# Modulation columns of the first four chunks from TensorE, for latents and context in one product

## The chip, the core and the metric

The kernel runs on one core of one Trainium2 chip. The metric is the time of one execution on the device in microseconds (us), and the figure of a kernel is the median of its runs.

## What is computed

Two layers of a diffusion backbone work on 1024 latent tokens and 256 context tokens of width 1024. What matters here is the beginning of layer 0: the modulation and the first product of its mixer.

```python
mod_lat = (silu_c @ ada_w[i] + ada_b[i])[:, None, :]
mod_ctx = (silu_cc @ ada_w[i] + ada_b[i])[None, None, :]
sh1, sc1, g1, sh2, sc2, g2 = jnp.split(mod_lat, 6, axis=-1)
csh1, csc1, cg1, csh2, csc2, cg2 = jnp.split(mod_ctx, 6, axis=-1)
h = modulate(rms_norm(x, norm_g[i, 0]), sh1, sc1)
hc = modulate(rms_norm(ctx, norm_g[i, 0]), csh1, csc1)
...
z = jax.nn.gelu(h @ w_in)
```

`modulate(h, shift, scale)` is `h * (1 + scale) + shift`. Shift and scale of layer 0 are two vector-matrix products of length 1024 with a matrix of 1024 x 2048 (the first two of the six parts of ada_w), once for the latents and once for the context. `h @ w_in` follows for 1280 rows and 4096 columns.

## The kernel before

The tokens are ten tiles of 128 rows: 0 to 7 are latents, 8 and 9 context. The first mixer is a gMLP, called for five tiles at a time. Its products run in the f32r type as three matmuls per piece: high part by high part, low by high, high by low (`mm3`). The width of 1024 is cut into eight chunks of 128, numbered k.

The program begins with a head (lines 676 to 780), which is written out by hand and whose instructions on VectorE, ScalarE, TensorE and the queue of SyncE keep the order of the code (`pins`, line 584). It normalizes the first five tiles of x and makes the first column block, 512 of the 2048 columns of the v half of `h @ w_in`. For each chunk k it does this:

- `flip_x(k)` (line 645): five 128x128 transposes on TensorE into a psA bank. Of the two psA buffers one holds a sum of the head all the time, so the next chunk's flip has to wait until `x_hi(k)` has read the other.
- The modulation columns of the chunk, one number per partition for shift and scale, written into `modc` by `finish_cols` on VectorE (line 198).
- `x_hi(k)` on ScalarE (line 651): scale, shift and the cast to the high part. `x_lo(k)` on VectorE (line 659): the low part.
- `head_mm(k, part)` (line 662) for parts 0 to 2: five 128x512 matmuls each, with the weights that `w_load`, `w_hi` and `w_lo` have loaded and split.

The columns come from `AdaBlock(k0, nk)` (line 588) for nk chunks at once: chunk 0, chunk 1, then pairs. The constructor loads the block's columns of ada_w in tiles "act" (six buffers), `accum` multiplies row block k by its 128 numbers of silu(c) and adds it up on VectorE, and `total` sums the result over the partitions with a matmul by a column of ones (`ones` in the rows), one per chunk and per shift or scale.

After the head `gmlp` (line 823) makes three more column blocks of four u steps each (30 matmuls of 128x512 per u step) and then the rest. Between its steps it takes steps of the generator `extra`, 1 or 2 per u step (18 in these three blocks) and two per feature block after that. The generator begins with the context's modulation, `ada_steps(0, 0, (1,))` and `ada_steps(0, 1, (1,))`. Each of these loads 1024x1024 of ada_w in eight steps of 512 KB into the three buffers "raw", which the weights of w_in use too, adds up on VectorE into `acc`, and ends with small matmuls or transposes and `finish_cols`: 9 steps each. Then come the gate `ada_steps(0, 2, (0, 1))` for both streams, which ends in matmuls with a matrix of ones (`ada_gate`, line 220), and sums for layer 1. In `between` run the preparations of small tables, such as `cwcols`, which are transposed into psA and copied by VectorE (`cols_of`, line 166). The order of these instructions on each engine is made by a scheduler.

Of the kernel before, what the change touches and what calls it, by code (L numbers as in the profile page):

```python
# [32 lines left out]
def hybrid_kernel(  # L33
# [23 lines left out]
    V, S, G, T = Engine(nc.vector, "V"), Engine(nc.scalar, "S"), Engine(nc.gpsimd, "G"), Engine(nc.tensor, "T")  # L57
# [23 lines left out]
    def t_raw():  # L81
        return sb.tile([P, 1024], F32, name=nm("raw"), tag="raw", bufs=3)
# [34 lines left out]
    def t_acc():  # L117
        return stage_pool["pool"].tile([P, 1024], F32, name=nm("acc"), tag="acc", bufs=2)
# [14 lines left out]
    def psB(shape=(P, 512)):  # L133
        return ps.tile(list(shape), F32, name=nm("psB"), tag="psB", bufs=4)
# [192 lines left out]
    def src_row(stage, t):  # L327
        if stage == 0:
            return x_in[0, t * P:(t + 1) * P, :] if t < 8 else ctx_in[0, (t - 8) * P:(t - 7) * P, :]
        return xs[stage][t * P:(t + 1) * P, :]  # L330
# [254 lines left out]
    pA0 = psA()  # L585
    pl0 = [psB() for _ in range(4)] + [pA0[:, 0, :]]

    class AdaBlock:
        def __init__(self, k0, nk):
            self.k0, self.nk = k0, nk  # L590
# [28 lines left out]
                             start=True, stop=True)  # L619

        def finish(self):
            k0, nk = self.k0, self.nk
            p = pts[k0][:, 1, 256:256 + 2 * nk]
            for s in (1, 0):
                finish_cols(0, s, 0, p[:, s * nk:(s + 1) * nk], slice(k0, k0 + nk))

    raws, w0, pts, tms = {}, {}, {}, {}

    def w_load(u, nb=0):
        raws[nb, u] = t_raw()  # L630
        Q.dma_start(raws[nb, u].rearrange("p (a b) -> p a b", a=2),
                    w_in[0][u * 256:u * 256 + 2 * P, E + nb * 512:E + nb * 512 + 512]
                    .rearrange("(k p) n -> p k n", p=P))

    def w_hi(u, nb=0):
        hi, lo = t_w("wh"), t_w("wl")
        w0[nb, u] = (hi.rearrange("p (a b) -> p a b", a=2), lo.rearrange("p (a b) -> p a b", a=2))
        S.copy(hi, raws[nb, u])
        raws[nb, u] = (raws[nb, u], hi, lo)

    def w_lo(u, nb=0):
        raw, hi, lo = raws.pop((nb, u))
        V.tensor_sub(lo, raw, hi)

    def flip_x(k):
        pts[k] = psA()
        for i in range(5):
            T.transpose(out=pts[k][:, i // 4, (i % 4) * P:(i % 4 + 1) * P], in_=xn0[:, i, k * P:(k + 1) * P],
                        identity=ident)

    def x_hi(k):
        pt, tm = pts[k], t_tmp()
        gg, sh = mod_cols(0, 1, 0)[:, k:k + 1], mod_cols(0, 0, 0)[:, k:k + 1]
        S.activation(tm[:, 0:512], pt[:, 0, :], AF.Identity, bias=sh, scale=gg)
        S.activation(tm[:, 512:640], pt[:, 1, 0:128], AF.Identity, bias=sh, scale=gg)
        S.copy(hk(hb0, 0, k)[:, 0:640], tm[:, 0:640])
        tms[k] = tm

    def x_lo(k):
        V.tensor_sub(hk(hb0, 1, k)[:, 0:640], tms[k][:, 0:640], hk(hb0, 0, k)[:, 0:640])  # L660

    def head_mm(k, part):
        wh, wl = w0[0, k // 2]
        a, b = ((0, 0), (0, 1), (1, 0))[part]
        for i in range(5):
            T.matmul(pl0[i], hk(hb0, b, k)[:, i * P:(i + 1) * P], (wh, wl)[a][:, k % 2, :],
                     start=(k == 0 and part == 0), stop=(k == KD - 1 and part == 2))
# [5 lines left out]
        V.tensor_copy(cl, p)  # L673
        return cl

    b0 = AdaBlock(0, 1)
    adab, aR = load_rows([ada_b.rearrange("l (k p) -> (l k) p", p=P)])
    ngr, nR = load_rows([norm_g.rearrange("l i (k p) -> (l i k) p", p=P)])
    for i, t in enumerate(LAT):
        Q.dma_start(xn0[:, i, :], src_row(0, t))  # L680
    w_load(0)
    b1 = AdaBlock(1, 1)
    abcols = cols_in(adab, aR, "abcols")
    ngcols = cols_in(ngr, nR, "ngcols")
    b0.accum(range(KD))
    for i, t in enumerate(LAT):
        r = rstd_of(xn0[:, i, :])
        V.tensor_scalar(out=xn0[:, i, :], in0=xn0[:, i, :], scalar1=r, scalar2=None, op0=ALU.mult)
    flip_x(0)
    b0.total()  # L690
    w_hi(0)
    b0.finish()
    x_hi(0)
    w_lo(0)
    flip_x(1)
    b1.accum(range(0, 4))
    x_lo(0)
    b2 = AdaBlock(2, 2)
    head_mm(0, 0)
    b1.accum(range(4, 8))  # L700
    b1.total()
    b2.accum(range(0, 2))
    b1.finish()
    head_mm(0, 1)
    head_mm(0, 2)
    x_hi(1)
    b2.accum(range(2, 4))
    w_load(1)
    b3 = AdaBlock(4, 2)
    flip_x(2)  # L710
    x_lo(1)
    w_hi(1)
    b2.accum(range(4, 7))
    head_mm(1, 0)
    head_mm(1, 1)
    w_lo(1)
    b2.accum(range(7, 8))
    b2.total()
    head_mm(1, 2)
    b3.accum(range(0, 1))  # L720
    b2.finish()
    x_hi(2)
    b3.accum(range(1, 3))
    x_lo(2)
    w_load(2)
    b4 = AdaBlock(6, 2)
    flip_x(3)
    x_hi(3)
    b3.accum(range(3, 5))
    x_lo(3)  # L730
    w_hi(2)
    head_mm(2, 0)
    head_mm(2, 1)
    head_mm(2, 2)
    flip_x(4)
    head_mm(3, 0)
    b3.accum(range(5, 7))
    w_lo(2)
    b3.accum(range(7, 8))
    head_mm(3, 1)  # L740
    b3.total()
    b4.accum(range(0, 1))
    b3.finish()
    head_mm(3, 2)
    x_hi(4)
    b4.accum(range(1, 3))
    x_lo(4)
    w_load(3)
    flip_x(5)
    x_hi(5)  # L750
    b4.accum(range(3, 5))
    x_lo(5)
    head_mm(4, 0)
    head_mm(4, 1)
    head_mm(4, 2)
    flip_x(6)
    w_hi(3)
    head_mm(5, 0)
    head_mm(5, 1)
    b4.accum(range(5, 8))  # L760
    b4.total()
    w_lo(3)
    b4.finish()
    head_mm(5, 2)
    x_hi(6)
    x_lo(6)
    w_load(0, 1)
    flip_x(7)
    x_hi(7)
# [848 lines left out]
    def pre_b0():  # L1618
# [1 line left out]
        return build(hold["h"], 0, 0, 0, [(0, 5 * P, 3 * P), (3 * P, SEQ, 256)], [], 640)  # L1620

    gmlp(0, hb0, LAT, gate_of(0, 2),
         chain(ada_steps(0, 0, (1,)), ada_steps(0, 1, (1,)), ada_steps(0, 2, (0, 1)), ada_steps(1, 3, (0,)),
               ada_steps(1, 4, (0,))),
         chain(more_cols(), prep_ws(), flip0()), pre_b0, head=(pl0, w0_next))

# [494 lines left out]
```

## Time and profile before

| | |
|---|---|
| three runs | 2856.6 us median (2850.05 to 2860.5) |
| profiled execution | 2860.88 us, its span 2859.1 us |
| granted clock of TensorE, mean | 0.988 |
| TensorE matmul busy | 2741.8 us, 96% |
| VectorE busy | 2221.8 us, 78% |
| ScalarE busy | 1391.2 us, 49% |
| moved by DMA | 537.13 MB |

The profile is one execution, recorded by instruction; the durations in the text are from it. PE is TensorE (PEld its weight loads), DVE VectorE, ACT ScalarE, POOL GpSimd, SP SyncE, and SPq is the queue of SyncE, which issues DMAs. A row of the timeline gives start, duration, engine, line, operation, output <- inputs, shapes and count; in brackets stands how long the engine was idle before and what ended that. Buffers carry the names of the code's tiles. Line 50 is the helper through which every instruction is made.

### The profile page before, as it was taken

Reading aid. Unit: us, or ns where it says so; the run is one execution under the profiler, and the core shown is the slowest. Engines: PE = TensorE matmul, PEld = TensorE weight load, DVE = VectorE, ACT = ScalarE, POOL = GpSimd, SP = SyncE. Lnnn points to the kernel's source line nnn. Section 1 sums busy time; section 2 is a strip of 40 time slices with the busy share of each in tenths; the row PEclk is TensorE's granted clock in tenths of the full one; section 3 lists DMA queues with packets and bytes.
Section 4 is the critical chain, followed back from the end, with each engine's and each line's share of the span. In section 5 each row is a group of like instructions: output and inputs, shape, how many; then the busy total and the mean of one; then the engine's idle time right before and its main releaser. Section 6 shows DMA issues by size and latency. Waiting matters only on the chain.

```text
span 2859.1 us, 40314 instructions
## 1 busy us (share of the span) xinstructions
PE 2741.8 (96%) x14570; PEld 2354.1 (82%) x14570; DVE 2221.8 (78%) x3466; ACT 1391.2 (49%) x2291; POOL 616.6 (22%) x806
## 2 busy tenths in 40 slices
PE   7999999999989999999999899999998999999998
PEld 5798887898889888888788778888887888888786
DVE  6567684787779899887776568898887788888776
ACT  4333242232367444455434545777876444445433
POOL 1164021360210212111000124543333121220000
PEclk9999999999999999999999999999999999999999
DMA  7775457554488355467855565347577345545753
GB/s 260 251 234 166 145 161 227 177 167 131 171 249 240 103 170 162 157 217 238 287 169 184 188 212 186 115 145 239 181 242 220 126 162 182 160 144 198 248 177 125
DMA packets 436335, 537.13 MB, mean 188 GB/s; under 512 B 20004, under 2 KB 300452, under 8 KB 436135
## 3 DMA queue, kind: packets, MB, share of 16 engines
q1 hardware_dynamic: 379575, 470.84, 51.4%
q10 hardware_dynamic: 55408, 59.52, 6.2%
q0 software_dynamic: 1152, 4.19, 0.4%
q8 instruction: 115, 1.88, 0.3%
q14 instruction: 85, 0.70, 0.1%
HBM read 414.40 MB, written 120.07 MB: 187 GB/s over the span
## 4 chain that ended last, share of the span: by engine, by line
PE 65%; DVE 13%; DMA 11%; ACT 5%; issue 4%; POOL 2%; SPq 1%; ACTq 0%; DVEq 0%; POOLq 0%
PE psB L50 48%; PE psA L50 16%; DVE row L50 3%; DVE wl L50 3%; DMA raw<-in_ada_w_dram 3%; DVE tmp L50 1%; DVE acc L50 1%; ACT wh L50 1%; ACT tmp L50 1%; DMA xT<-row 1%; DMA raw<-in_a_w_in_dram 1%; DVE y L50 1%; POOL sm L50 1%; DMA raw<-in_f_w_up_dram 1%; DMA raw<-in_f_w_down_dram 1%
## 5 line engine op out<-in xcount | busy, mean ns | idle before, releaser
L50 PE MATMUL psB<-cmb,wh 128*128 128x512 f32 (+2 forms) x2584 | 750.3, 374 | 7.2 <-ACT row L50 6.2
L50 PEld LDWEIGHTS psB<-cmb,wh 128*128 128x128 f32 x2584 | 471.9, 188 | 98.4 <-ACT row L50 8.1
L50 PE MATMUL psB<-cmb,wl 128*128 128x512 f32 (+2 forms) x1292 | 483.2, 374 | 0.2 <-DVE wl L50 0.2
L50 ACT CAST wh<-raw 128x1024 fp32r<-128x1024 f32 (+1 forms) x313 | 265.1, 863 | 441.6 <-PE psB L50 165.5
L50 DVE TENSOR_TENSOR wl<-raw,wh 128x1024 fp32r<-128x1024 f32 (+1 forms) x313 | 307.6, 997 | 106.6 <-ACT wh L50 104.9
L50 PEld LDWEIGHTS psB<-cmb,wl 128*128 128x128 f32 x1292 | 243.2, 188 | 44.0 <-DVE wl L50 0.8
L50 PE MATMUL psB<-wh,big 128*128 128x512 f32 x816 | 271.1, 398 | 3.7 <-ACT big L50 1.3
L50 ACT CAST wh<-row 128x1024 fp32r<-128x1024 f32 (+1 forms) x196 | 162.5, 834 | 186.8 <-DVE row L50 92.3
L50 PE MATMUL psB<-wh,act 128*128 128x512 f32 x640 | 200.1, 390 | 0.8 <-DVE tmp L50 0.8
L50 DVE TENSOR_TENSOR wl<-row,wh 128x1024 fp32r<-128x1024 f32 (+1 forms) x196 | 185.2, 948 | 12.2 <-ACT wh L50 11.8
L50 PE MATMUL psA<-big,wh 128*128 128x320 f32 x1024 | 193.2, 310 | 0.3 <-ACT row L50 0.3
L50 POOL TENSOR_TENSOR row<-raw,raw 128x512 f32<-128x512 f32 x44 | 68.5, 1558 | 574.2 <-DMA raw<-in_f_w_up_dram 490.8
L50 PEld LDWEIGHTS psB<-wh,big 128*128 128x128 f32 x816 | 154.3, 190 | 39.9 <-ACT tmp L50 2.4
L50 DVE SCALAR_TENSOR_TENSOR acc<-raw,ccols,acc 128x1024 f32<-128x1024 f32 x98 | 126.7, 1311 | 75.8 <-DMA raw<-in_ada_w_dram 75.5
L50 DVE SCALAR_TENSOR_TENSOR row<-row,cwcols,row 128x1024 f32<-128x1024 f32 (+2 forms) x142 | 152.6, 1075 | 39.2 <-ACT row L50 22.7
L50 ACT CAST ah<-raw 128x1024 fp32r<-128x1024 f32 x80 | 77.6, 974 | 201.6 <-PE psB L50 80.8
L50 DVE TENSOR_TENSOR row<-row,row 128x512 f32<-128x512 f32 (+4 forms) x169 | 155.9, 926 | 19.9 <-DMA row<-actd 12.2
L50 POOL TENSOR_SCALAR row<-row,sm,sm 128x128 f32<-128x128 f32 x160 | 144.1, 919 | 115.2 <-DMA row<-vscr 99.3
L50 PEld LDWEIGHTS psA<-big,wh 128*128 128x128 f32 x1024 | 159.9, 188 | 0.7 <-ACT row L50 0.5
L50 PE MATMUL psB<-wl,big 128*128 128x512 f32 x408 | 157.2, 395 | 0.9 <-DVE wl L50 0.9
L50 DVE TENSOR_TENSOR al<-raw,ah 128x1024 fp32r<-128x1024 f32 x80 | 90.2, 1128 | 71.9 <-ACT ah L50 71.6
L50 PE MATMUL psB<-row,wh 128*128 128x256 f32 x744 | 136.9, 286 | 8.2 <-ACT wh L50 6.7
(279 smaller groups left out, 6226.0 us busy)
## 6 DMA issues: line engine op xcount, KB each, us to landing
raw<-in_f_w_up_dram SPq DMA_DIRECT2D x121, 512.0 KB, 4.8
raw<-in_ada_w_dram SPq DMA_DIRECT2D x88, 512.0 KB, 4.4
raw<-in_a_w_in_dram SPq DMA_DIRECT2D x64, 512.0 KB, 4.8
wh<-woscr SPq DMA_DIRECT2D x48, 512.0 KB, 4.1
row<-actd SPq DMA_DIRECT2D x44, 512.0 KB, 5.5
actc<-row SPq DMA_DIRECT2D x44, 512.0 KB, 4.1
raw<-actc SPq DMA_DIRECT2D x40, 512.0 KB, 3.6
actd<-row SPq DMA_DIRECT2D x39, 512.0 KB, 2.7
```

The costliest lines, as they stand in the source:

```text
L50: ins = fn(*a, **kw)
```

## The change

Four things change.

The columns of chunks 0 to 3 come from the new `AdaColumn(k0)`, one chunk each. It loads the chunk's columns of ada_w in two tiles of 512 KB (scale first). Its `total` is 8 matmuls for scale and 8 for shift, which add up over the row blocks in PSUM: the stationary operand is a 128x128 piece of ada_w, the moving one two columns, silu(c) and silu(c_ctx) of that row block. So the context's columns of these chunks come out of the same products; `finish(1)` writes them. Chunks 4 to 7 keep `AdaBlock` in two pairs.

In the code of the head ada_b, norm_g and x are loaded ahead of the first column's tiles, and the calls stand in another order. `w_hi(0)` casts in two halves, behind `x_hi(0)`.

The context's part of the generator is now `ctx_steps()`, which sums only columns 512 to 1023 of shift and scale, both in one accumulator: 9 steps where there were 18. All that follows in the generator comes nine steps earlier.

```diff
+    def ctx_steps():
+        acc = t_acc()
+        for k in range(KD):
+            raw = t_raw()
+            for m in range(2):
+                Q.dma_start(raw[:, m * 512:(m + 1) * 512], ada_w[0, k * P:(k + 1) * P, m * D + 512:(m + 1) * D])
+            cc = ccols[:, KD + k:KD + k + 1]
+            if k == 0:
+                V.tensor_scalar(out=acc, in0=raw, scalar1=cc, scalar2=None, op0=ALU.mult)
+            else:
+                V.scalar_tensor_tensor(out=acc, in0=raw, scalar=cc, in1=acc, op0=ALU.mult, op1=ALU.add)
+            yield
+        p = psB()
+        for k in range(KD):
+            T.matmul(p[:, k:k + 1], acc[:, k * P:(k + 1) * P], ones[:, 0:1], start=True, stop=True)
+        for m in range(2):
+            finish_cols(0, m, 1, p[:, 4 * m:4 * m + 4], slice(4, KD))
+        yield
...
+    class AdaColumn:
+        def __init__(self, k0):
+            self.k0, self.nk, self.rv = k0, 1, {}
+            for s in (1, 0):
+                self.rv[s] = t_act((P, KD, P), F32)
+                Q.dma_start(self.rv[s], ada_w[0, :, s * D + k0 * P:s * D + (k0 + 1) * P]
+                            .rearrange("(k p) n -> p k n", p=P))
+
+        def total(self):
+            p = pts[self.k0][:, 1, 256:260]
+            both = ccols.rearrange("p (s k) -> p s k", k=KD)
+            for s in (1, 0):
+                for k in range(KD):
+                    T.matmul(p[:, 2 * s:2 * s + 2], self.rv[s][:, k, :], both[:, :, k], start=(k == 0), stop=(k == KD - 1))
+
+        def finish(self, stream=0):
+            p = pts[self.k0][:, 1, 256:260]
+            for s in (1, 0):
+                finish_cols(0, s, stream, p[:, 2 * s + stream:2 * s + stream + 1], slice(self.k0, self.k0 + 1))
...
-        S.copy(hi, raws[nb, u])
+        for c in ((0, 512), (512, 1024)) if (nb, u) == (0, 0) else ((0, 1024),):
+            S.copy(hi[:, slice(*c)], raws[nb, u][:, slice(*c)])
...
-    b0 = AdaBlock(0, 1)
     adab, aR = load_rows([ada_b.rearrange("l (k p) -> (l k) p", p=P)])
     ngr, nR = load_rows([norm_g.rearrange("l i (k p) -> (l i k) p", p=P)])
     for i, t in enumerate(LAT):
         Q.dma_start(xn0[:, i, :], src_row(0, t))
+    b0 = AdaColumn(0)
     w_load(0)
-    b1 = AdaBlock(1, 1)
+    b1 = AdaColumn(1)
+    b2 = AdaColumn(2)
...
-         chain(ada_steps(0, 0, (1,)), ada_steps(0, 1, (1,)), ada_steps(0, 2, (0, 1)), ada_steps(1, 3, (0,)),
+         chain(ctx_steps(), ada_steps(0, 2, (0, 1)), ada_steps(1, 3, (0,)),
                ada_steps(1, 4, (0,))),
```

What this does to the order of the instructions is shown at three places. The first is TensorE at the beginning of the head. `ident,y` are the transposes of a chunk, the products of 128x1 or 128x2 are the columns, and the 128x512 ones are a part of `head_mm`. Before:

```order
L50 MATMUL psA_186<-ident,y_109 128x128 x5
L50 MATMUL psA_186<-ones,acc_121 128x1 x2
L50 MATMUL psA_208<-ident,y_109 128x128 x5
L50 MATMUL psB_111<-wh_196,big_205 128x512
L50 MATMUL psB_112<-wh_196,big_205 128x512
L50 MATMUL psB_113<-wh_196,big_205 128x512
L50 MATMUL psB_114<-wh_196,big_205 128x512
L50 MATMUL psA_110<-wh_196,big_205 128x512
L50 MATMUL psA_208<-ones,acc_139 128x1 x2
```

And now:

```order
L50 MATMUL psA_176<-ident,y_109 128x128 x5
L50 MATMUL psA_176<-ccols,act_124 128x2 x8
L50 MATMUL psA_176<-ccols,act_126 128x2 x8
L50 MATMUL psB_111<-wh_211,big_204 128x512
L50 MATMUL psB_112<-wh_211,big_204 128x512
L50 MATMUL psB_113<-wh_211,big_204 128x512
L50 MATMUL psB_114<-wh_211,big_204 128x512
L50 MATMUL psA_110<-wh_211,big_204 128x512
L50 MATMUL psA_229<-ident,y_109 128x128 x5
L50 MATMUL psA_229<-ccols,act_130 128x2 x8
L50 MATMUL psA_229<-ccols,act_132 128x2 x8
```

Sixteen products stand where two stood, ahead of the first wide matmul and again behind it, and the second chunk's transposes have moved behind the first five wide matmuls.

The second place is VectorE near the end of the second column block, around the last copy of `cwcols`, whose psA buffer the third block's sum takes next. Products `acc<-raw,ccols` are steps of the modulation sums, each waiting for a load. Before:

```order
L50 SCALAR_TENSOR_TENSOR acc_608<-raw_885,ccols,acc_608 128x1024
L50 COPY cwcols_696<-psA_694 128x66
L50 TENSOR_TENSOR wl_833<-raw_830,wh_832 128x1024
L50 TENSOR_SCALAR acc_942<-raw_943,ccols 128x1024
L50 BN_STATS st_538<-tmp_752 128x6
L50 BN_STATS st_538<-tmp_756 128x6
L50 BN_STATS st_538<-tmp_760 128x6
L50 COPY cwcols_739<-psA_737 128x66
```

And now:

```order
L50 SCALAR_TENSOR_TENSOR acc_645<-raw_870,ccols,acc_645 128x1024
L50 COPY cwcols_736<-psA_734 128x66
L50 TENSOR_TENSOR wl_877<-raw_874,wh_876 128x1024
L50 SCALAR_TENSOR_TENSOR acc_645<-raw_929,ccols,acc_645 128x1024
L50 BN_STATS st_575<-tmp_795 128x6
L50 BN_STATS st_575<-tmp_799 128x6
L50 BN_STATS st_575<-tmp_803 128x6
L50 COPY cwcols_780<-psA_778 128x66
```

The last copy has a sum ahead of it in both; before it was the first of the next set, now it is the last of the context's.

The third place is TensorE at the end of the fourth column block. `psA<-ident,row` are transposes of a token tile, and `psA<-big` begins the next part of the gMLP. Before:

```order
L50 MATMUL psA_1029<-wh_1159,big_485 128x512
L50 MATMUL psA_1254<-ident,row_1193 128x128 x8
L50 MATMUL psB_1270<-ident,acc_942 128x128 x4
L50 MATMUL psB_1276<-ident,acc_942 128x128 x4
L50 MATMUL psA_1321<-big_205,wh_1219 128x320 x2
```

And now:

```order
L50 MATMUL psA_1080<-wh_1213,big_512 128x512
L50 MATMUL psA_1309<-ident,row_1247 128x128 x8
L50 MATMUL psB_1334<-wh_1330,ones 128x512
L50 MATMUL psB_1334<-wl_1331,ones 128x512
L50 MATMUL psB_1338<-wh_1330,ones 128x512
L50 MATMUL psB_1338<-wl_1331,ones 128x512
```

Where the transposes of the context's scale sums stood, the gate's matmuls stand now, which need the high and low parts of its sums.

More of the change, by code (lines that the diff above doesn't have):

```diff
@@ L586, in hybrid_kernel, with finish_block @@
     pl0 = [psB() for _ in range(4)] + [pA0[:, 0, :]]
+    def finish_block(block):
+        k0, nk = block.k0, block.nk
+        p = pts[k0][:, 1, 256:256 + 2 * nk]
+        for s in (1, 0):
+            finish_cols(0, s, 0, p[:, s * nk:(s + 1) * nk], slice(k0, k0 + nk))
     class AdaBlock:
@@ L621, in finish @@
         def finish(self):
-            k0, nk = self.k0, self.nk
-            p = pts[k0][:, 1, 256:256 + 2 * nk]
+            finish_block(self)
+    class AdaColumn:
+        def __init__(self, k0):
+            self.k0, self.nk, self.rv = k0, 1, {}
             for s in (1, 0):
-                finish_cols(0, s, 0, p[:, s * nk:(s + 1) * nk], slice(k0, k0 + nk))
+                self.rv[s] = t_act((P, KD, P), F32)
[11 more added lines that the diff above has]
+                finish_cols(0, s, stream, p[:, 2 * s + stream:2 * s + stream + 1], slice(self.k0, self.k0 + 1))
     raws, w0, pts, tms = {}, {}, {}, {}
@@ L680, in hybrid_kernel @@
         Q.dma_start(xn0[:, i, :], src_row(0, t))
+    b0 = AdaColumn(0)
     w_load(0)
-    b1 = AdaBlock(1, 1)
+    b1 = AdaColumn(1)
+    b2 = AdaColumn(2)
     abcols = cols_in(adab, aR, "abcols")
     ngcols = cols_in(ngr, nR, "ngcols")
-    b0.accum(range(KD))
     for i, t in enumerate(LAT):
@@ L690, in hybrid_kernel @@
     b0.total()
-    w_hi(0)
     b0.finish()
     x_hi(0)
+    b0.finish(1)
+    w_hi(0)
+    x_lo(0)
     w_lo(0)
+    b3 = AdaColumn(3)
+    w_load(1)
+    head_mm(0, 0)
     flip_x(1)
[L696 to L700, printed above, removed]
     b1.total()
-    b2.accum(range(0, 2))
     b1.finish()
+    x_hi(1)
+    b1.finish(1)
     head_mm(0, 1)
     head_mm(0, 2)
[L706 to L709, printed above, removed]
+    x_lo(1)
+    b4 = AdaBlock(4, 2)
     flip_x(2)
-    x_lo(1)
+    b2.total()
+    b2.finish()
+    x_hi(2)
+    b2.finish(1)
     w_hi(1)
-    b2.accum(range(4, 7))
+    b4.accum(range(0, 2))
     head_mm(1, 0)
     head_mm(1, 1)
+    head_mm(1, 2)
+    x_lo(2)
     w_lo(1)
[L717 to L724, printed above, removed]
     w_load(2)
-    b4 = AdaBlock(6, 2)
+    b6 = AdaBlock(6, 2)
     flip_x(3)
+    b3.total()
+    b3.finish()
     x_hi(3)
-    b3.accum(range(3, 5))
-    x_lo(3)
-    w_hi(2)
+    b3.finish(1)
+    b4.accum(range(2, 4))
     head_mm(2, 0)
@@ L734, in hybrid_kernel @@
     head_mm(2, 2)
+    x_lo(3)
+    b4.accum(range(4, 8))
+    w_hi(2)
     flip_x(4)
     head_mm(3, 0)
-    b3.accum(range(5, 7))
+    head_mm(3, 1)
+    b4.total()
+    b4.finish()
+    x_hi(4)
     w_lo(2)
[L739 to L743, printed above, removed]
     head_mm(3, 2)
-    x_hi(4)
-    b4.accum(range(1, 3))
     x_lo(4)
+    b6.accum(range(0, 2))
     w_load(3)
@@ L750, in hybrid_kernel @@
     x_hi(5)
-    b4.accum(range(3, 5))
     x_lo(5)
+    b6.accum(range(2, 5))
     head_mm(4, 0)
@@ L757, in hybrid_kernel @@
     w_hi(3)
+    b6.accum(range(5, 8))
     head_mm(5, 0)
+    b6.total()
+    b6.finish()
+    x_hi(6)
+    w_lo(3)
+    x_lo(6)
     head_mm(5, 1)
[L760 to L763, printed above, removed]
     head_mm(5, 2)
-    x_hi(6)
-    x_lo(6)
     w_load(0, 1)
```

## Prediction

> **What bounds the kernel now.** I began with the page's span and busy times, and went on to the waits of TensorE and to the table by stage.
>
> ```profile
> span 2859.1 us, 40314 instructions
> PE 2741.8 (96%) x14570; PEld 2354.1 (82%) x14570; DVE 2221.8 (78%) x3466; ACT 1391.2 (49%) x2291; POOL 616.6 (22%) x806
> ```
> ```profile
> PE psA L50 <- DVE cwcols L50: 4.6, 1, 4.6
> PE psB L50 <- DVE tmp L50: 2.8, 4, 0.9
> PE psB L50 <- DVE wl L50: 1.7, 2, 1.1
> PE psB L50 <- DVE y L50: 1.3, 1, 1.3
> PE psA L50 <- ACT row L50: 0.3, 1, 0.3
> ```
> ```profile
> 23.00:32.00 9.00, 7.77 (x20) 5.78 (x21) 8.16 (x17) 2.82 (x5) 0.00 (x0) 1.00 0.94 318
> 32.00:66.00 34.00, 32.45 (x164) 25.67 (x163) 26.26 (x42) 17.27 (x25) 0.00 (x0) 1.00 0.67 217
> 96.00:104.00 8.00, 3.48 (x9) 2.81 (x10) 3.60 (x6) 0.00 (x0) 0.00 (x0) 0.79 0.65 223
> ```
> TensorE is busy 96% of the span, so work added to it lengthens the kernel unless it falls where TensorE idles. The second view (us waited, times, longest) covers 60 to 400 us: 10.7 us of waits in all, 4.6 of them one wait for the copy of cwcols. The third (stretch, length, busy us of PE, weight loads, DVE, ACT, POOL, then granted clock, DMA share, GB/s) shows that from 32 to 66 us, where the change puts its matmuls, TensorE works 32.45 of 34 us. There is little idle time there to take anything in. The two kernels issue the same sequences again from about the end of the first gMLP call (some 400 us), so the sum is over 0 to 400 us. Next, the timeline of TensorE in and behind the head (start, us, operation, instructions).
>
> ```profile
> 19.44 0.47 PE L50 MATMUL psA<-ident,y 128*128 128x128 f32 x1 [0.99 <-DVE y L50]
> 19.71 0.85 PE L50 MATMUL psA<-ones,acc 128*128 128x1 f32 x4
> 20.43 1.31 PE L50 MATMUL psA<-ident,y 128*128 128x128 f32 x5
> 23.08 2.08 PE L50 MATMUL psB<-wh,big 128*128 128x512 f32 x4 [1.34 <-ACT big L50]
> 24.95 0.63 PE L50 MATMUL psA<-wh,big 128*128 128x512 f32 x1
> 26.73 1.02 PE L50 MATMUL psA<-ones,acc 128*128 128x1 f32 x4 [1.15 <-DVE acc L50]
> 27.61 2.05 PE L50 MATMUL psB<-wh,big 128*128 128x512 f32 x4
> 33.65 1.09 PE L50 MATMUL psB<-wh,big 128*128 128x512 f32 x4
> 34.57 0.40 PE L50 MATMUL psA<-wh,big 128*128 128x512 f32 x1
> 45.08 0.95 PE L50 MATMUL psA<-ones,acc 128*128 128x1 f32 x8
> 45.88 1.17 PE L50 MATMUL psB<-wl,big 128*128 128x512 f32 x4
> 65.07 0.39 PE L50 MATMUL psA<-wl,big 128*128 128x512 f32 x1
> 100.52 0.79 PE L50 MATMUL psA<-wh,big 128*128 128x512 f32 x1 [4.58 <-DVE cwcols L50]
> 103.60 0.40 PE L50 MATMUL psB<-wl,big 128*128 128x512 f32 x1
> 127.67 1.95 PE L50 MATMUL psB<-ones,acc 128*128 128x1 f32 x16
> 129.48 0.48 PE L50 MATMUL psB<-wl,big 128*128 128x512 f32 x1
> ```
> Paces are read from start to start. A 128x512 matmul takes (24.95-23.08)/4 = 0.47 us early and (34.57-33.65)/4 = 0.23 later: TensorE starts at half pace (the granted clock column reads 1.00 there, so only the pace shows it). Every 128x128 by 128x1 product in f32 is two instructions. One costs (45.88-45.08)/8 = 0.10 or (129.48-127.67)/16 = 0.113 at full pace, and 0.18 (19.71 to 20.43) to 0.22 (26.73 to 27.61) at half. The head's last matmul starts at 65.07.
>
> **The head, part by part.** The other engines' rows, ScalarE first, then VectorE, then the queue of SyncE:
>
> ```profile
> 9.96 1.06 ACT L50 ACTIVATE tmp<-y 128x1024 bf16<-128x1024 f32 x1 [5.60 <-DMA y<-in_x_dram]
> 17.15 1.04 ACT L50 CAST wh<-raw 128x1024 fp32r<-128x1024 f32 x1
> 21.14 1.13 ACT L50 ACTIVATE tmp<-psA,modc 128x512 f32<-128x512 f32 x2 [2.94 <-DVE modc L50]
> 22.30 0.72 ACT L50 CAST big<-tmp 128x640 fp32r<-128x640 f32 x1
> ```
> ```profile
> 36.55 1.53 DVE L50 SCALAR_TENSOR_TENSOR acc<-act,ccols,acc 128x512 f32<-128x512 f32 x2
> 91.39 1.28 DVE L50 SCALAR_TENSOR_TENSOR acc<-raw,ccols,acc 128x1024 f32<-128x1024 f32 x1 [4.12 <-DMA raw<-in_ada_w_dram]
> 97.80 0.75 DVE L50 TENSOR_SCALAR acc<-raw,ccols 128x1024 f32<-128x1024 f32 x1 [3.86 <-DMA raw<-in_ada_w_dram]
> 100.26 0.21 DVE L50 COPY cwcols<-psA 128x66 f32<-128x66 f32 x1
> 163.74 1.28 DVE L50 SCALAR_TENSOR_TENSOR acc<-raw,ccols,acc 128x1024 f32<-128x1024 f32 x1 [5.10 <-DMA raw<-in_ada_w_dram]
> 222.54 1.23 DVE L50 TENSOR_TENSOR wl<-acc,wh 128x1024 fp32r<-128x1024 f32 x1 [3.40 <-ACT wh L50]
> ```
> ```profile
> 1.52 2.05 SPq L50 DMA_DIRECT2D act<-in_ada_w_dram x4
> 3.62 0.50 SPq L50 DMA_DIRECT2D tmp<-in_ada_b_dram  x1
> 4.16 0.59 SPq L50 DMA_DIRECT2D tmp<-in_norm_g_dram  x1
> 4.79 3.15 SPq L50 DMA_DIRECT2D y<-in_x_dram  x5
> ```
> Earlier x. ScalarE begins on the first tile of x at 9.96, after 5.60 us of waiting for its load. The four loads of ada_w (2.05 us of issue, 1 MB) no longer stand ahead of ada_b, norm_g and x on SyncE, so x is issued 2.1 us earlier. At the 318 GB/s of the table that megabyte takes 3.3 us, so the last transpose of flip_x(0) comes 2.1 to 3.3 us earlier: 16.1 to 17.3, I take 16.6. GpSimd's memset and selects of the mask now stand between the first x tiles' statistics; they are over before the last tile, so nothing.
>
> First column. b0's sums on VectorE go (eight, beside waiting). In their place TensorE does 16 products, 32 instructions, at half pace 0.18 to 0.22: 6.4 us, to 23.0. As many bytes as before stand ahead of these tiles, which landed under x's time then, so no wait for them. From the end of the small products to the first 128x512 there were 23.08-20.43 = 2.65 us; now the half cast of wh comes behind x_hi(0) (1.04/2), so 3.2. head_mm(0, 0) then starts at 26.2 and not 23.08: **+3.1** (between +2 and +4).
>
> The other columns. Behind head_mm(0, 0) there were 4 + 3 x 8 = 28 small instructions. Now there are 3 x 32 + 2 x 8 = 112. 84 more at 0.10 to 0.113 are 8.4 to 9.5 us: **+9.0**. TensorE is in order and nearly gapless here, so nothing hides them. What they take off VectorE had only made TensorE wait 1.15 us at 26.73.
>
> Half pace. Before, 15 matmuls of 0.47 instead of 0.23 and some small ones lost 3.8 us. Full pace came at about 31.9, 5.2 us after the last gap. Now it finds 5 wide matmuls, a flip and some small products: 0 to 3.6 lost, I take 2.0: **-1.8**. The Trainium skill, page "TensorE: Matmul & The Clock Gate", Part 1, says that the array leaves half rate after one window of about 3.4 us of sustained work. By that rule the 6.4 us of the first column would already raise the clock, and the sum would be 2 us lower; no run so far shows whether such small products count as work.
>
> Waits. The waits of 1.15 at 26.73 and of about half a us each at flips fall (some 2.2 us). A new one comes: b6.total now stands behind one part of head_mm(5), and six sums of 1.53/2 us stand between x_lo(5) and it on VectorE. TensorE gets there 5.0 us after flip_x(5) (four parts of 1.14, one flip), VectorE in 3.0 + 4.5 = 7.5 (the 3.0 are a flip of 0.5, 1.13 and 0.72 on ScalarE and a difference of under 1): 2.5 us. **0** together. Context's three short operations per column, the earlier tables of ada_b and norm_g, and w_load(1) ahead of the two-column blocks have slack of microseconds on their engines.
>
> Head: 3.1 + 9.0 - 1.8 = **+10.3 us** (+6.5 to +12).
>
> **Behind the head.** Context's sums: 16 loads of 512 KB and 16 sums (1.28 each) become 8 steps, each still one 512 KB buffer, in two DMAs. VectorE gains 10 us, TensorE loses eight transposes, about **-0.9**. The wait at 95.9 us: it costs 4.58 and a slow restart: 7 matmuls in 103.60-100.52 = 3.08 us instead of 1.6, so 6.1. The copy that ends it stands behind an ada_w sum that waited 3.86 us for its load; in the new order one such sum still stands ahead of it, of 1.28 rather than 0.75. Eight ada_w loads through the three buffers come ahead of the copy instead of nine. Between all 6.1 gone and 1.5 more, I take **-2.5**. The gate of ada 2: it moves by nine steps to the end of the fourth column block. Its hi and lo need the last two sums (1.28 each), two casts and two differences (1.23 each). Before, the last sum there ran at 163.74 after 5.10 us of waiting for a load, and the transposes hardly waited. In-order TensorE would now wait between 0 and 4.6 us; **+1.5**. Waits from 166 to 400 us: 6.1 us, and the later steps find VectorE less loaded; at best all go, at worst 2 more come: **-1.5**.
>
> Sum: 10.3 - 0.9 - 2.5 + 1.5 - 1.5 = +6.9 us. The profiled execution took 2860.9 us (span 2859.1 and 1.8 around), so 2867.8; the median of the three runs, 2856.6, lies 4.3 lower, so the forecast is **2863.5 us**, 0.24% more. A measurement of this kernel can tell about 0.5% (14.3 us) from no change: this is no change by that measure.
>
> **The rivals.** A: the small products are paid for. The long wait goes whole with its restart (-6.1), those behind 166 us too (-6.1), the gate is hidden, the transposes go (-0.9), and the head comes out at its low end, +6.5: -6.6, or 2850. For: half the bytes of context's sums. Against: a sum still stands ahead of the copy.
>
> B: slower, TensorE stays at half pace. If streams of one- and two-column products do not count as work, four columns of them between the wide parts could hold the pace down until the last column. The place is from head_mm(0, 0) to head_mm(2, 0), it decides if the pace is still 0.47 at head_mm(1, 0). Price: 30 wide matmuls by 0.24 and 96 small ones by 0.09 are 15.8, of which 2.0 are counted: +13.8, 2877.3, slower by 0.7%. For: the early transposes and small products did not raise the pace before 31.9. Against: ten wide ones from 27.6 on did.
>
> C: the small products hide. Weight loads overlap matmuls; in 32 to 66 us they were busy 25.67 of 34. If most of the 9.0 went beside the wide ones, the head would be +3 and the sum 2856. Against: the eight at 45.08 took their 0.80 us between two wide groups in full.
>
> **How the numbers follow.** The forecast has 0.64 (its own range 2857 to 2871), A 0.14, B 0.10, C 0.12. The range 2850 to 2873 holds forecast, A and C but for their edges, and leaves B out. Faster by over 0.5% (under 2842.3) needs more than A: 0.02. Slower by over 0.5% (above 2870.9) is most of B and the forecast's edge: 0.12. Within: 0.86.
>
> **What would show it.** Right: in the new trace the first 128x512 matmul starts near 26 us, each column's 32 instructions take 3.2 to 3.6 us at full pace, and the head ends near 75 us. The wait for cwcols is there, shorter. Wrong: a head that ends before 70, small products of far less than 0.10 us, wide matmuls at 0.47 beyond 35 us (B), or a difference that arises behind 400 us, where I expect none.

## The result and the profile after

| | before | after |
|---|---|---|
| median of the timed runs | 2851.1 us (6 runs, 2846.2 to 2860.5) | 2875.4 us (6 runs, 2873.9 to 2881.3) |
| profiled execution, its span | 2860.9, 2859.1 us | 2875.3, 2873.5 us |

The changed kernel takes 1.0085 times as long (interval 1.0065 to 1.0104): 24.3 us more, slower by 0.85%. The forecast was +6.9 us and "no change"; the time lies above the range.

I read the new trace in the order of the prediction. First TensorE in the head (start, us, operation, instructions, idle time before it):

```profile
16.40 0.47 PE L50 MATMUL psA<-ident,y 128*128 128x128 f32 x1 [0.99 <-DVE y L50]
16.67 6.83 PE L50 MATMUL psA<-ccols,act 128*128 128x2 f32 x32
26.52 2.07 PE L50 MATMUL psB<-wh,big 128*128 128x512 f32 x4 [3.03 <-ACT wh L50]
28.40 0.63 PE L50 MATMUL psA<-wh,big 128*128 128x512 f32 x1
29.89 6.82 PE L50 MATMUL psA<-ccols,act 128*128 128x2 f32 x32
36.57 2.05 PE L50 MATMUL psB<-wh,big 128*128 128x512 f32 x4
42.04 3.71 PE L50 MATMUL psA<-ccols,act 128*128 128x2 f32 x32
45.62 2.05 PE L50 MATMUL psB<-wh,big 128*128 128x512 f32 x4
47.47 0.63 PE L50 MATMUL psA<-wh,big 128*128 128x512 f32 x1
51.26 3.63 PE L50 MATMUL psA<-ccols,act 128*128 128x2 f32 x32
54.76 1.17 PE L50 MATMUL psB<-wh,big 128*128 128x512 f32 x4
56.10 1.91 PE L50 MATMUL psB<-wh,big 128*128 128x512 f32 x4
73.63 1.05 PE L50 MATMUL psA<-ones,acc 128*128 128x1 f32 x8 [2.05 <-DVE acc L50]
84.06 0.39 PE L50 MATMUL psA<-wl,big 128*128 128x512 f32 x1
```

The beginning is as forecast: last transpose at 16.40, first wide matmul at 26.52. But the second column still takes 36.57-29.89 = 6.68 us, 0.21 an instruction, so half pace. The wide matmuls of the first chunk behind it are at half pace too. The third column is at full pace (45.62-42.04 = 3.58 us, 0.11 each), and right behind it the wide ones take (47.47-45.62)/4 = 0.46 us again. The same comes once more behind the fourth column, at 56.10. The head's last matmul starts at 84.06 instead of 65.07: +19.0 us.

The stretches of the same trace say why (stretch, length, busy us and instructions of PE, weight loads, DVE, ACT, POOL, then granted clock, DMA share, GB/s):

```profile
42.00:45.40 3.40, 3.40 (x33) 3.40 (x31) 0.00 (x0) 0.00 (x0) 0.00 (x0) 1.00 0.07 14
45.40:48.80 3.40, 3.40 (x12) 2.72 (x12) 1.66 (x8) 2.47 (x4) 0.00 (x0) 0.53 0.90 283
55.60:59.00 3.40, 3.40 (x10) 2.71 (x9) 2.32 (x6) 2.65 (x4) 0.00 (x0) 0.54 0.87 275
```

From 42.0 to 45.4 us TensorE does nothing but small products, without a gap. In the next 3.4 us the granted clock is 0.53. So the clock falls although the engine never idles.

Next, four of the nine rows of its waits from 60 to 400 us (us in all, times, longest), and the two places of the timeline that the prediction spoke of, with the longest wait last:

```profile
PE psB L50 <- DVE tmp L50: 7.3, 6, 3.9
PE psA L50 <- DVE acc L50: 2.0, 1, 2.0
PE psA L50 <- DVE wl L50: 1.6, 1, 1.6
PE psA L50 <- DVE cwcols L50: 0.4, 1, 0.4
```
```profile
116.87 0.50 PE L50 MATMUL psA<-wh,big 128*128 128x512 f32 x1 [0.41 <-DVE cwcols L50]
179.78 0.50 PE L50 MATMUL psB<-wh,ones 128*128 128x512 f32 x1 [0.35 <-ACT tmp L50]
181.31 0.50 PE L50 MATMUL psB<-wh,ones 128*128 128x512 f32 x1 [0.31 <-ACT tmp L50]
193.32 0.56 PE L50 MATMUL psA<-big,wl 128*128 128x320 f32 x2 [1.61 <-DVE wl L50]
264.18 1.09 PE L50 MATMUL psB<-ident,acc 128*128 128x128 f32 x4 [3.87 <-DVE tmp L50]
```

The wait for cwcols is 0.41 us where it was 4.58, and the gate costs 0.66. But there are new waits, one of 0.95 us at 112.98 and more from 156 us on, the longest before the transposes of a later sum.

How far the new trace lies behind the old one is read off matmuls that are the same in both (start in the trace named, less the start in the profiled execution of before). The columns to the right belong to experiments below:

| near (us, before) | after | e10 (128 columns) | e12 (steps not shifted) | e13 (both) | e14 | e11 (sums alone) |
|---|---|---|---|---|---|---|
| 25, head_mm(0, 0) | 3.4 | 1.2 | 3.3 | 2.9 | 0.1 | 0.1 |
| 65, end of the head | 19.0 | 10.8 | 16.0 | 14.8 | 10.7 | 0.2 |
| 101, behind cwcols | 16.4 | 8.0 | 13.7 | 12.5 | 6.6 | -0.2 |
| 166, fourth block done | 16.7 | 7.9 | 10.3 | 9.1 | 3.3 | 3.1 |
| 230 | 20.9 | 11.6 | 8.2 | 6.9 | 1.7 | 7.0 |
| 262 | 25.5 | 15.8 | 8.3 | 6.9 | 1.7 | 11.5 |
| 420, end of the stage | 20.3 | 10.5 | 8.1 | 6.2 | -0.2 | 6.3 |

Between 166 and 262 us the changed kernel loses 8.8 us more, and by 420 it has 5.2 of them back; the kernel before still has waits there (1.34 us at 292.94) and the changed one none behind 264. Behind 420 us the order is the same in both kernels.

### The profile page after: what moved, and what is told of

Same layout as the page of the kernel before. It is cut to its first block, busy times and chain, and to the rows that moved or that the text cites. A ratio compares the mean times of both kernels' runs of the same rounds, so it can differ in the third digit from the quotient of the medians.

```text
span 2873.5 us, 40466 instructions
## 1 busy us (share of the span) xinstructions
PE 2755.8 (96%) x14674; PEld 2367.0 (82%) x14674; DVE 2204.0 (77%) x3447; ACT 1390.6 (48%) x2292; POOL 604.0 (21%) x806
## 5 line engine op out<-in xcount | busy, mean ns | idle before, releaser
L50 DVE SCALAR_TENSOR_TENSOR acc<-raw,ccols,acc 128x1024 f32<-128x1024 f32 x91 | 118.5, 1321 | 61.6 <-DMA raw<-in_ada_w_dram 61.5
L50 POOL TENSOR_SCALAR row<-row,sm,sm 128x128 f32<-128x128 f32 x160 | 130.2, 827 | 131.0 <-DMA row<-vscr 69.8
L50 PEld LDWEIGHTS psB<-wh,act 128*128 128x128 f32 x640 | 120.1, 188 | 28.9 <-issue 3.5
```

The lines of the kernel that those rows point to most:

```text
L50: ins = fn(*a, **kw)
```

## The experiments

Two theories stood at first. Clock: streams of one- and two-column products let TensorE's clock fall, and cost the head some 8 us beyond their own time. Work: every small product is paid at its price, and nothing else. Beside them: that a part of the loss is made behind the head. All times are medians; the ratio is to the kernel before on the same chip. Its median beside the runs was between 2851.0 and 2854.7 us, so runs are best compared by how far each lies above it; for the changed kernel that is 24.3 us.

**e1: the small products spread.** The 16 products of columns 1 to 3 come through a generator between the wide matmuls:

```diff
-    head_mm(0, 0)
+    head_mm(0, 0, b1.gen, 4)
     flip_x(1)
-    b1.total()
...
-    head_mm(0, 1)
-    head_mm(0, 2)
+    head_mm(0, 1, b2.gen, 2)
+    head_mm(0, 2, b2.gen, 2)
```

> The changed kernel with the same matmuls in another order: the small products of columns 1 to 3 no longer stand in a stretch of 32 instructions, but two to eight at a time between the wide matmuls of the chunk before (into a free bank, so that they need not wait for the transposes). Clock theory: it is the stretches that take the granted clock away, so the half-pace windows at 45.4 to 48.8 and 55.6 to 59.0 us go and full pace comes before 42 us; the head's last matmul starts at 75 to 80 instead of 84.1, and the time is 2866 to 2871. Work theory (112 small instructions in order, wherever they stand): the head ends at 83 to 85 and the time stays at 2875, within 2 us.

Measured: 2886.5 us (1.0108, 1.0090 to 1.0127), 32.5 us above the kernel before, 8 more than the changed kernel. Its timeline:

```profile
37.15 0.85 PE L50 MATMUL psA<-ccols,act 128*128 128x2 f32 x4
38.43 0.85 PE L50 MATMUL psA<-ccols,act 128*128 128x2 f32 x4
56.56 0.42 PE L50 MATMUL psA<-ccols,act 128*128 128x2 f32 x2
57.41 0.42 PE L50 MATMUL psA<-ccols,act 128*128 128x2 f32 x2
64.65 1.08 PE L50 MATMUL psB<-wh,big 128*128 128x512 f32 x4
65.56 0.39 PE L50 MATMUL psA<-wh,big 128*128 128x512 f32 x1
```

Neither theory had this. Two products and a wide matmul take 1.28 us (37.15 to 38.43) and one product and a wide matmul 0.85 (56.56 to 57.41), where at full pace they would be 0.67 and 0.45. So it goes from 26.5 to 63 us, and full pace, (65.56-64.65)/4 = 0.23 us, comes when the small ones are gone. The work theory falls, and so does my form of the clock theory, in which it is the stretches that do it. A wide matmul has some 0.43 us of the 0.85, a good half, and still the clock does not rise. So it is not the stretches as such, but how little of the wide ones there is.

**e2: a warm start.** Idle TensorE is given 14 wide matmuls ahead of the first transpose, and four behind each of the first four; the result is overwritten.

```diff
+    spin(14)
     adab, aR = load_rows([ada_b.rearrange("l (k p) -> (l k) p", p=P)])
...
+            if k == 0 and i < 4:
+                spin(4)
```

> The changed kernel with 30 more wide matmuls whose result is overwritten: 14 of them ahead of the first transpose, where TensorE idles, and four behind each of the first four transposes, where it waits for tiles of x. Clock theory: the first column's 32 instructions find full pace (3.5 us instead of 6.8), head_mm(0, 0) starts at 23 to 24 instead of 26.5, one window of half pace follows the stretch, and the second column is at full pace again: the head ends at 74 to 78, the time is 2865 to 2870. Rival, that the pace early in the head is low for another reason than the clock (small products of 0.21 us because their operands just landed): the small products keep 0.21 us, and the time is 2875 or, by the added work, up to 2880.

Measured: 2872.7 us (1.0066, 1.0053 to 1.0080), 18.8 us above the kernel before. Rows of its head:

```profile
17.33 3.63 PE L50 MATMUL psA<-ccols,act 128*128 128x2 f32 x32
23.99 2.07 PE L50 MATMUL psB<-wh,big 128*128 128x512 f32 x4 [3.03 <-ACT wh L50]
35.60 4.55 PE L50 MATMUL psA<-ccols,act 128*128 128x2 f32 x32
79.50 0.39 PE L50 MATMUL psA<-wl,big 128*128 128x512 f32 x1
```

The small products take 0.11 at once, so their 0.21 was the clock. Behind the stretch the wide ones are at half pace, and the third column falls into a drop itself (4.55 us). The head ends at 79.5, 4.6 us earlier but short of the 74 to 78 that I gave.

**e3 and e4: one half of the change each.** e3 is the kernel before with `ctx_steps()`; context's first four columns take the latents' totals. e4 is the changed kernel with context's sums as before:

```diff
                 finish_cols(0, s, 0, p[:, s * nk:(s + 1) * nk], slice(k0, k0 + nk))
+                if k0 < 4:
+                    finish_cols(0, s, 1, p[:, s * nk:(s + 1) * nk], slice(k0, k0 + nk))
```
```diff
-         chain(ctx_steps(), ada_steps(0, 2, (0, 1)), ada_steps(1, 3, (0,)),
+         chain(ada_steps(0, 0, (1,)), ada_steps(0, 1, (1,)), ada_steps(0, 2, (0, 1)), ada_steps(1, 3, (0,)),
```

> The kernel before with only the second half of the change: context's sums halved, the head as it was (context's first four columns then take the latents' totals, so their numbers are not the reference's). Theory that the loss is made in the head: 2845 to 2851, no slower than before, since the long wait at 96 us shrinks or goes. Rival, that a part of the loss is made behind the head by the moved steps (gate of ada 2, the wait of 3.9 us at 264 us): 2855 to 2860.

> The changed kernel with context's sums as before (all columns, twice the bytes), so the head's part of the change alone. Theory that the loss is made in the head: the head ends at 84 us as in the changed kernel, 19 later than before, and the time is 2868 to 2877. Rival, that half of the loss is made behind the head: 2860 to 2865.

Measured: e4 2878.1 us (1.0090, 1.0074 to 1.0106), as much as the whole change; e3 2867.6 us (1.0052, 1.0039 to 1.0065), 13.6 us slower where I expected no loss. The two add up to 38 us, the change costs 24. So halving context's sums, with the steps behind them moved up, is a loss on the old head and none on the new. In e3 the head had three more VectorE operations per column, so it was tried again.

**e9, e10: the same instructions, with 128 columns.** Each small product streams both columns 64 times; one of each is used.

```diff
-                    T.matmul(p[:, 2 * s:2 * s + 2], self.rv[s][:, k, :], both[:, :, k], start=(k == 0), stop=(k == KD - 1))
+                    T.matmul(p[:, 128 * s:128 * s + 128].rearrange("p (s n) -> p s n", s=2), self.rv[s][:, k, :],
+                             both[:, :, k:k + 1].to_broadcast([P, 2, 64]), start=(k == 0), stop=(k == KD - 1))
```

> The changed kernel with the same instructions at the same places, but each small product streams 128 columns instead of two (context's and the latents' column each repeated 64 times; one of each is used). Theory that the granted clock follows what TensorE streams, so that one- and two-column products do not count as work: the second column is at full pace or nearly, there are no half-pace windows behind the columns, the head's last matmul starts at 72 to 78 and not at 84.1, and the time is 2863 to 2870, although nothing was taken away; if an instruction of 128 columns takes longer than one of two at full pace (a transpose of 128 columns takes 0.09), that eats a part. Theory that the pace is low because of the count of small instructions or of their f32 weights: pace and head as in the changed kernel, 2875 or more.

```profile
16.52 5.40 PE L50 MATMUL psA<-ccols,act 128*128 128x128 f32 x32
24.96 1.19 PE L50 MATMUL psB<-wh,big 128*128 128x512 f32 x4 [3.03 <-ACT wh L50]
26.77 3.74 PE L50 MATMUL psA<-ccols,act 128*128 128x128 f32 x32
30.27 1.17 PE L50 MATMUL psB<-wh,big 128*128 128x512 f32 x4
75.69 0.39 PE L50 MATMUL psA<-wl,big 128*128 128x512 f32 x1
```
```profile
20.00:54.00 34.00, 29.86 (x201) 26.39 (x200) 14.89 (x43) 10.67 (x17) 0.00 (x0) 1.00 0.80 251
```

This is the run that decides. Nothing is taken away, and each product streams 64 times as much; a column still takes 30.27-26.77 = 3.50 us, as with two columns. But the clock rises within the first column (5.40 us in place of 6.83) and stays at 1.00 from 20 to 54 us, where there are three more columns. The granted clock column also reads 1.00 ahead of a kernel's first full pace, so here the paces are the proof: 3.50 us for the second column instead of 6.68, and 1.19 us for the first four wide matmuls instead of 2.07. The head ends at 75.69, 8.4 us earlier. Two windows of half pace are left in this head (54.2 to 57.6 and 64.4 to 67.8 us), behind waits of 1.10 and 1.60 us for VectorE's sums. TensorE's clock follows what streams through it, and an instruction of one or two columns is next to nothing by that measure, although it takes half of the time of a wide one.

The median, though, was 2873.6 us (1.0078, 1.0060 to 1.0096). That is 18.9 above the kernel before, 5.4 less than the changed kernel and not 8. So both ran again, side by side:

> The changed kernel once more, unaltered, so that the next two stand beside it on one chip. Any theory: 2873 to 2878, and the half-pace windows in the head at other places or as before, since the windows do not start with the kernel.

> The kernel with 128 columns streamed once more, on the same chip as the changed kernel. In its profile it was 8.3 us ahead at 420 us and only 1.8 in the medians. If the 8 us of the head hold to the end: 5 to 9 us below the changed kernel of this call. If later waits take them back: 0 to 3 us below.

Measured: the changed kernel 2876.0 us (1.0084, 1.0071 to 1.0097), the one with 128 columns 2867.2 (1.0049, 1.0036 to 1.0062): 8.8 us less. The gain of the head holds to the end here. In the first profile it was 8.3 us at 420 us as well, and was lost behind that, where both kernels issue the same order. Single executions differ there by more than this: e9 and e10 are one kernel, and from 420 us to the end e9's execution falls back by 3.4 us against the profiled one of before, while e10's gains 11.1. What makes that spread stays open.

**e8: a warm start for the kernel before**, with the same 30 matmuls as e2.

> The kernel before with 30 more wide matmuls whose result is overwritten, 14 ahead of the first transpose and four behind each of the first four. Clock theory: of the 3.8 us that half pace costs there, 1 to 3.5 go: the head ends at 62 to 64 instead of 65.1, and the time is 2 to 4 us below the kernel before (about 2850 to 2852). Rival, that half pace early in the head hides in the waits for VectorE's sums (1.15 us at 26.73): no change within 1 us.

Measured: 2857.8 us (1.0011, 1.0001 to 1.0022), slower. Two rows of VectorE and one of TensorE:

```profile
11.27 0.26 DVE L50 COPY abcols<-psA 128x96 f32<-128x96 f32 x1 [6.14 <-PE psA L50]
```
```profile
29.58 0.61 PE L50 MATMUL psA<-ones,acc 128*128 128x1 f32 x4 [2.22 <-DVE acc L50]
```

The 14 matmuls stood ahead of the tables' transposes, so `abcols` came at 11.27 instead of 8.42, and with it b0's sums and x: my edit cost 3 us there. At full pace TensorE then waits 2.22 us for VectorE's sums instead of 1.15. The old head was paced by VectorE, and half pace mostly hid behind it; in the new one VectorE is relieved and half pace is paid in full. That is a reading of the rows and not shown; a kernel before with a better placed warm start was not tried.

**e5 and e7: the price of small products.** 192 products (384 instructions, result unused) are put into column blocks two to four of the kernel before: in e5 as stretches of 8, 16 and 24, in e7 one to three behind every third wide matmul.

```diff
+                    if head and nb and k:
+                        for _ in range((0,8,16,24)[nb]):
+                            T.matmul(pA[:, 1, 0:(0,1,1,1)[nb]], ident, ones[:, 0:(0,1,1,1)[nb]], start=True, stop=True)
```
```diff
+                        n, j = (0, 8, 16, 24)[nb] if head else 0, 5 * k + i
+                        for _ in range(n * (j + 1) // 10 - n * j // 10):
+                            T.matmul(pA[:, 1, 0:1], ident, ones[:, 0:1], start=True, stop=True)
```

> The kernel before with stretches of small f32 products (128x1, result unused) in the dense part behind the head: 8 products in each of the four quarters of the second column block, 16 in the third, 24 in the fourth; 384 instructions. Work theory: 384 by 0.11 = 42 us more, less up to 6 us of waits that they cover: 2890 to 2896, no half-pace windows. Clock theory: stretches of 3.5 and 5.3 us each bring a window of half pace or two (1.7 us each on the wide matmuls, about as much again on small ones inside it): 14 to 25 us more than that, 2905 to 2920; the stretches of 1.8 us bring none or few.

> The same 192 small products in the same blocks, but one to three at a time behind every third wide matmul; by time at full pace the wide ones then have 79, 66 and 56 parts in 100 of the three blocks. Work theory: as with the stretches, 2890 to 2896. Clock theory, by share of wide work (two products per wide one held half pace from 36 to 60 us in the woven head): no half pace in the second block; where it begins in the others shows the share that is needed; if the whole fourth block falls to half pace, about 25 us more than the work, else 2890 to 2896, 15 to 25 us less than the stretches.

Measured: e5 2915.7 us (1.0222, 1.0203 to 1.0241), e7 2892.2 (1.0138, 1.0123 to 1.0153). First e5, then e7, in stretches:

```profile
66.00:100.00 34.00, 34.00 (x184) 29.12 (x183) 19.18 (x21) 8.91 (x12) 0.00 (x0) 1.00 0.77 251
100.00:133.00 33.00, 33.00 (x175) 27.83 (x173) 16.67 (x31) 6.03 (x9) 0.00 (x0) 0.90 0.51 164
133.00:166.00 33.00, 33.00 (x162) 29.09 (x163) 10.50 (x12) 9.18 (x15) 6.97 (x9) 0.74 0.55 184
166.00:222.00 56.00, 56.00 (x294) 49.40 (x294) 7.77 (x8) 10.15 (x16) 4.27 (x7) 0.79 0.37 107
```
```profile
66.00:100.00 34.00, 34.00 (x180) 28.97 (x180) 19.93 (x23) 9.33 (x14) 0.00 (x0) 1.00 0.80 258
104.00:132.00 28.00, 28.00 (x164) 23.98 (x163) 15.13 (x27) 4.38 (x6) 0.75 (x3) 1.00 0.52 159
144.40:151.20 6.80, 6.80 (x27) 6.13 (x26) 2.15 (x3) 0.89 (x2) 0.00 (x0) 0.50 0.63 204
152.00:196.00 44.00, 44.00 (x290) 39.66 (x290) 7.08 (x7) 11.71 (x18) 6.64 (x9) 1.00 0.40 114
```

The same products cost 37.6 us spread out and 61 in stretches: 23.5 us between the two is order alone. In e5 the missing clock (one less the granted clock, times the length) is 0.10 x 33 + 0.26 x 33 + 0.21 x 56 = 23.6 us, in e7 0.5 x 6.8 = 3.4; that is 20 of the 23.5. The added stretches of 1.8 us bring no drop, those of 3.6 and 5.4 us do. Spread products bring none, with 79, 66 or, in the fourth block (the last row), 56 parts in 100 of the time for the wide ones. The one drop in e7, at 144.4, stands behind a stretch of the kernel's own, 16 small instructions from 141.40 on (1.88 us). The kernel before has that stretch too, at 127.67, and its clock is half from 130.8 to 134.2. So a stretch of under 2 us can be enough.

**e11 and e12: the moved steps.** e11 is e3 with the old head but for two copies. e12 is the changed kernel with nine empty steps behind context's sums, so that the steps of ada 2, 3 and 4 stand where they stood before:

```diff
             finish_cols(0, m, 1, p[:, 4 * m:4 * m + 4], slice(4, KD))
+            V.tensor_copy(mod_cols(0, m, 1)[:, 0:4], mod_cols(0, m, 0)[:, 0:4])
```
```diff
             finish_cols(0, m, 1, p[:, 4 * m:4 * m + 4], slice(4, KD))
-        yield
+        for _ in range(10):
+            yield
```

> Only the halved sums of context, now with the head of before instruction for instruction but for two copies (context's first four columns are copies of the latents', so the numbers are not the reference's). If the 13 us that the sums cost with the three more operations per column in the head came from those and from the pace there: 2852 to 2858, the head's last matmul at 65 to 66.5. If they come from the moved steps behind the head: 2862 to 2868 again, with the difference between 65 and 300 us.

> The changed kernel with nine empty steps behind context's sums, so that the later steps (gate of ada 2, ada 3, ada 4) stand where they stood before. If the shift by nine steps makes the wait of 3.9 us at 264 us: that wait goes, the one that before had near 300 us comes back (about 2.4), net 2 to 3 us faster at 420 us, and the gate's place costs nothing either way. If the wait comes from elsewhere: no difference.

Measured: e11 2865.6 us (1.0042, 1.0026 to 1.0057), e12 2865.6 (1.0053, 1.0040 to 1.0065), 10.4 below the changed kernel measured beside it. Waits of TensorE from 60 to 400 us in e11, and in e12:

```profile
PE psB L50 <- DVE tmp L50: 5.6, 3, 3.9
PE psA L50 <- DVE cwcols L50: 4.3, 1, 4.3
```
```profile
PE psB L50 <- DVE tmp L50: 1.0, 2, 0.7
```

In the table above e11 has the old head (+0.2), loses nothing to 101 us and 11.7 from there to 262. It is the moved steps. The wait of 3.9 us before the transposes is there in both kernels with shifted steps and gone in e12, which from 101 to 420 us even gains 5.6 us on before. I had expected 2 to 3 us from e12; it was the whole stretch from 130 us on and not the one wait. Why the moved steps cost so much there is a reading: ahead of the wait of 3.87 us in the changed kernel, VectorE itself stood 4.52 and 3.54 us for loads of such sums, with what TensorE needs behind them in its order. The later of the two:

```profile
252.75 1.29 DVE L50 SCALAR_TENSOR_TENSOR acc<-raw,ccols,acc 128x1024 f32<-128x1024 f32 x1 [3.54 <-DMA raw<-in_ada_w_dram]
```

e4 and e12 both have the new head, and their later steps stand at the same places; the sums are whole in e4 and halved in e12. e4 lies 24.2 us above the kernel before, e12 14.6. So halving the sums is itself a gain there, of some 10 us, and the shift takes it away. The cwcols wait of 4.3 us is still there in e11, with half the sums, and gone in e4, with whole sums and the new head: in the changed kernel it shrank because TensorE comes later, and not because the sums are halved.

**e13 and e14: both undone.** e13 has the 128 columns and the nine empty steps. e14 adds 10 wide matmuls behind the tables' transposes, four behind each of the first four transposes, and sets `b6.total()` behind `head_mm(5, 1)`:

```diff
     ngcols = cols_in(ngr, nR, "ngcols")
+    spin(10)
...
     head_mm(5, 0)
+    head_mm(5, 1)
     b6.total()
...
-    head_mm(5, 1)
     head_mm(5, 2)
```

> The changed kernel with 128 columns streamed and with the nine empty steps. If the two losses are separate (pace in the head 7 to 9 us, shifted steps behind it 8 to 10 us), both gains add: 16 to 19 us below the changed kernel, 2857 to 2861, within 8 us of the kernel before. If they overlap (a head that ends earlier meets the waits that the longer one covered): 2863 to 2867, no better than either alone.

> That kernel with two more edits: 10 wide matmuls whose result is overwritten behind the tables' transposes and four behind each of the first four transposes (now not ahead of the tables, which cost 3 us elsewhere), and the last column block's total one part of the head later. First column 3.5 instead of 5.4 us, the wait of 1.6 to 2.0 us at the total 1 us shorter and with luck its window of half pace (1.7 us) gone: 2 to 5 us below the kernel with the two edits alone, 2853 to 2858, level with the kernel before. If the first column's pace hides elsewhere: no difference to the two edits alone.

Measured: e13 2857.6 us (1.0024, 1.0014 to 1.0034), e14 2853.1 (1.0006, 0.9997 to 1.0015). The two losses are separate and add: 18.4 us back of the 25.0 that the changed kernel lost when it was measured again, and with the rest of the head's half pace and wait 23 of 25. e14 is level with the kernel before; no version here beats it. e14's first column and its total:

```profile
16.43 3.74 PE L50 MATMUL psA<-ccols,act 128*128 128x128 f32 x32
64.17 1.05 PE L50 MATMUL psA<-ones,acc 128*128 128x1 f32 x8 [0.88 <-DVE acc L50]
```

## Why the prediction was wrong, point by point

- **Start of the head: right.** First wide matmul at 26.52 (26.2 forecast), last transpose at 16.40 (16.6).
- **Added small products: right in price.** 0.11 us each at full pace, nothing hidden; rival C falls, and A with it.
- **"Half pace ... -1.8": this step failed.** I took it that full pace, once it came, would stay, and would come after a few us. In place of 2.0 us lost behind the start of the head, the rows show some 30 wide matmuls at 0.43 to 0.46 instead of 0.23 (6.6 us), a column at 6.7 instead of 3.5 and two sets of transposes at 1.06 instead of 0.47: about 11. Before it was 3.8, so the term is +7 and not -1.8, which is all of the 8.7 us between +19.0 and +10.3. With the pace mended (e9) the head is at +10.6, though partly by an earlier start (24.96).
- **Rival B had the mechanism, and 0.10.** It said the pace would be held down until the last column, and asked for 0.47 at head_mm(1, 0). The row there reads 0.46. In fact the clock comes and goes in windows of 3.4 us. What I held against it, that ten wide matmuls had raised the pace before, was true and no argument: a stretch of small products takes the pace away again. That B's sum, 2877.3, lies within 2 us of the result is luck: it has 15.8 us of half pace where the rows have 11, and nothing for the moved steps.
- **The Trainium skill's rule**, page "TensorE: Matmul & The Clock Gate", Part 1 (half rate left after one window of about 3.4 us of sustained work, and back after an idle one). The drops of 3.4 us agree with its window. That small products count as work, which I drew from it, does not hold: 6.8 us of them did not raise the clock, and 3.4 us of them without a gap (42.00 to 45.40) lost it.
- **The wait at b6's total: right in size** (2.05 against 2.5).
- **Behind the head: -3.4 forecast, +1.3 measured** (19.0 to 20.3). This failed as well. The wait for cwcols went nearly whole (0.41 left of 4.58; with the new wait of 0.95 the stretch from 65 to 101 us gives -2.6), for a reason that I did not give: TensorE comes later. The gate cost 0.66 and not 1.5. What I missed is that all later steps move up by nine and that this has a price of its own. The term "-1.5" for the waits from 166 us on, for which I let the later steps find VectorE less loaded, came out as +3.6 (16.7 to 20.3). In the profiles the shift costs 9 us from 65 to 420 us (+1.3 with it, -7.9 in e12; in the second profile of the changed kernel, -1.4, it costs 6.5).
- **The base.** The forecast started from the profiled execution and the median of three, 2856.6 us. The median of six is 2851.1, so the step is 17.4 us larger than forecast, although the time is only 11.9 above it: 5.5 us of the miss are hidden by a base that I took too high. Head 8.7 and behind it 4.7 make up 13.4 of the 17.4. The other 4.0 lie between the profiled execution of before and its median, and no trace shows where; from 420 us to the end that execution loses 5.9 us on that of after, in the same order of instructions.

## What to carry to other kernels

Before moving reductions onto TensorE as one-column products, count their time at half pace too, and what follows them at half pace: it is not how long TensorE is busy that keeps its clock up but how much it streams, and here 128 columns took no longer than two. Where a generator's steps are interleaved with other work, a shorter generator moves every later step up; pad it, and try it, before blaming the work. A wait for work of another engine shrinks when TensorE comes later, so a gain there may be only the loss ahead of it.

## What the runs showed of the hardware

- With 16 f32 products of 128x128 by 128 columns instead of two, the time was the same (3.50 us for 32 instructions), and the granted clock was 1.00 instead of falling.
- The drops of the granted clock last 3.4 us or a multiple. They do not start with the kernel: the changed kernel, run again, had them at other places and ended its head within 0.2 us of the first time. Rows of that second run, in which the clock was half from 39.8 to 46.6:

```profile
33.00:36.40 3.40, 3.40 (x11) 2.79 (x11) 1.24 (x7) 1.85 (x3) 0.00 (x0) 0.52 0.85 275
39.80:46.60 6.80, 6.80 (x25) 5.93 (x25) 2.67 (x10) 2.80 (x4) 0.00 (x0) 0.51 0.63 189
```

- Wide matmuls with a good half of the time did not raise the clock at half pace (e1), and with 56 parts in 100 they held it at full pace (e7). How much is needed can be counted in the 16 traces, window by window of 3.41 us from the first recorded change of the clock to 420 us (1823 windows). Count the moving columns that TensorE streams, those of f32 products and transposes twice, since 128 of them take 0.109 us where 512 columns of a wide matmul take 0.227. That is an estimate from these traces: some six wide matmuls per window, of the 15 that a window holds at full pace.
- In the changed kernel the window from 42.2 us on has about 120 columns and the one from 52.4 on 2300, and both are followed by half clock; the one from 49.0 on has 4900 and is not. In e1 the windows of the woven part, counted back from its first change at 63.85, have 760 to 3030. In e7's fourth block they have 4000 and more.
